# Attention's queries kept negated and scaled, and the sample's score products given two banks and a longer lag

## The chip, the core and the metric

The kernel runs on one core of a Trainium2 chip. The profile names the core's engines: PE (TensorE, the matmuls; PEld are its weight loads), DVE (VectorE), ACT (ScalarE), POOL (GpSimd) and SP (which here issues DMAs). Each engine works through its own list of instructions in a fixed order; an instruction that waits holds up all that stand behind it on its engine. The metric is the device time of one execution in microseconds (us); lower is better.

## The reference

One layer of a hybrid decoder for a prompt of 2048 tokens and for eight sample sequences with one new token each. Cut to what matters here:

```
h  = rms_norm(x) @ w_in                    # split into attention, indexer and recurrence parts
aq = rms_norm(aq, q_norm_g)                # 8 heads of 64; ak likewise with 2 heads
scores = sum_h relu(iq_h . ik) * iw_h      # indexer; keep the 256 best causal keys of each query
logits = (aq . ak_sel) * 64 ** -0.5        # masked where not chosen
att = softmax(logits) @ av_sel
x = x + concat(att, rec) @ w_out           # rec: a gated linear recurrence
x = x + square(relu(rms_norm(x) @ w_up)) @ w_down
```

For the samples the indexer scores 16384 cached keys of each of the eight sequences, picks 256 and gathers their keys and values.

## The kernel before

The prompt is 16 tiles of 128 rows (`NB`); the samples are one tile of 8 rows. The program runs in stages, and the trace shows their bounds:

- 0 to 1030 us: input projection, indexer scores of the prompt and the recurrence.
- Then three groups of tiles (0 to 4, 5 to 10, 11 to 15 with the samples). Each has an attention stage (from about 1030, 1885 and 2720 us) and an MLP stage with the output projection (from about 1280, 2095 and 2980 us). The first attention stage also holds the recurrence's share of the output projection.
- Beside the first two MLP stages run side tracks, generators advanced by so many matmul columns of the MLP (`PACE`, `PUMP`): the choice of the prompt's keys (`search_signs`, `choose`), and the samples' work (`sample`). The samples' indexer scores are all beside the first MLP stage, their choice, gathering and attention beside the second.

Products that need more than one pass are made of a high part and the rest: `wh`/`wl`, `uh`/`ul`, `kh`/`kl` and so on. ACT writes the high part, DVE (or POOL) subtracts it to get the low part.

**Prompt attention.** `logits` takes one head against all keys of a block in pieces of 512. Two matmuls make a piece in PSUM (`lg`, two banks); one DVE instruction adds the mask `MB`, writes `L` and carries the running maximum `mx`, which the core of the loop says:

```
front["dve"] = nc.vector.tensor_tensor_reduce(out=L[:, k0:k0 + kn], in0=ps[:, :kn], in1=MB[:, k0:k0 + kn],
                               scale=1.0, scalar=NEG if mx is None else mx,
                               op0=OP.add, op1=OP.max, accum_out=m2)
...
nm = p2.tile([P, 1], F32, tag="nm", name="nm", bufs=4)
nc.vector.tensor_scalar(nm, mx, -ATT_SCALE, None, op0=OP.mult)
nc.scalar.activation(L[:, :n], L[:, :n], AF.Exp, bias=nm, scale=ATT_SCALE, accum_out=sm[:, j:j + 1])
```

So each head of a block (16 blocks, 8 heads: 128 times) has a DVE instruction on one column (`nm`, L1001) between its last piece (L995) and its exponential on ACT (L1002). `values` then transposes `L` on PE (`pt`), splits it (`ph` on ACT, `pl` on DVE) and multiplies with the values (`O`).

**The samples' scores.** There are 32 units (8 sequences, 4 groups `u`). A unit gathers keys (`kg`, POOL), transposes them on DVE (`kt`, L1271) and makes four pieces: `kh` on ACT (L1282), `kl` on DVE (L1283), which `products` multiplies with the queries on PE (L1230), two matmuls a piece, summed over the four pieces in one PSUM bank `sc`. After that `weigh` copies half the bank on ACT (`rs`, L1237), adds the other half on DVE (`rs`, L1238), makes `rw` (L1239, L1240) and multiplies by the head weights (`wq`, L1242). `products` of a piece are written `LAG` pieces after its conversion; `kh` and `kl` have `LAG + 1` buffers; `sc` has `QS` banks. A bank is written anew only when the `rs` instructions of the unit that held it are done.

`LAG` also sets the delay of the products `lp` that build the samples' lists of keys (beside the second MLP stage), and `QS` the banks of other small products of the samples.

The order of instructions on every engine is made by a scheduler when the program is built, from priorities and the program's order, so a small edit moves many rows.

Of the kernel before, what the change touches and what calls it, by code (L numbers as in the profile page):

```python
# [8 lines left out]
F32 = mybir.dt.float32  # L9
# [8 lines left out]
OP = mybir.AluOpType  # L18
# [27 lines left out]
def hymba_kernel(ctx, tc, x_prompt, x_sample, cache_k, cache_v, cache_kidx, state_hgrn, page_table,  # L46
# [274 lines left out]
    def attn_proj(pc, p1, pr):  # L321
# [11 lines left out]
            nc.sync.dma_start(gains[:, i], src.to_broadcast([P, HD]))  # L333
        qg, kg, ig = (gains[:, i] for i in range(3))

        def load_weights(name, pieces):
            cols = sum(c for _, c in pieces)
            wh = p1.tile([P, 8, cols], F32R, name=f"wh_{name}")
            wl = p1.tile([P, 8, cols], F32R, name=f"wl_{name}")
            for q in range(4):  # L340
                raw = pr.tile([P, 2, 512], F32, tag="raw", name="raw", bufs=RB)
                d0 = 0
                for c0, c in pieces:
                    nc.sync.dma_start(raw[:, :, d0:d0 + c],
                                      w_in[0, q * 2 * P:(q + 1) * 2 * P, c0:c0 + c].rearrange("(k p) c -> p k c", p=P))
                    d0 += c
                s = slice(2 * q, 2 * q + 2)
                nc.scalar.copy(wh[:, s], raw[:, :, :cols])
                nc.vector.tensor_tensor(wl[:, s], raw[:, :, :cols], wh[:, s].bitcast(F32), op=OP.subtract)
            return wh, wl, cols  # L350
# [53 lines left out]
        def project_tile(t, po, q1, IK, hh, hl, i):  # L404
            n = rows(t)
            rs = slice(row0(t), row0(t) + n)
            for kind, (wh, wl, cols) in (("kiq"[i], weights[i]),):
# [3 lines left out]
                def post():  # L411
# [37 lines left out]
                            store(nv_sample[0].rearrange("b o k d -> (b o) (k d)"), o[:n, 128:256])  # L449
                            store(ni_sample[0].rearrange("b o d -> (b o) d"), o[:n, 256:320])  # L450
                    elif kind == "q":
                        head_norm(po, ps[:n], n, NH, qg, o[:n])
                        if t == NB:
                            store(aqD[rs], o[:n])
                            return
                        sp = split_heads(po, o, NH, "aqs", 1, nc.gpsimd)
                        for q in range(0, NH, 4):
                            pq = q1.tile([P, 512], F32, tag="ikt", name="aqt", bufs=2)
                            for j in range(4):
                                transpose_part(pq[:, j * P:(j + 1) * P], sp[:, q + j].rearrange("p a d -> p (a d)"))  # L460
                            qt = po.tile([P, 512], F32, tag="qt", name="qt", bufs=2)
                            (nc.vector.tensor_copy if q else nc.scalar.copy)(qt, pq)
                            store(qsD[t, :, q:q + 4], qt.rearrange("p (h t) -> p h t", t=P))
                    else:
                        nc.scalar.copy(o[:n], ps[:n])
                        store(iqD[rs], o[:n])
# [47 lines left out]
    def choose_keys(px):  # L514
# [25 lines left out]
        def choose(b, S, R):  # L540

            n = (b + 1) * P
            ngt, need = (small(x) for x in ("ngt", "need"))
            eq = px.tile([P, SEQ], BF, tag="eq", name="eq", bufs=1)
            nc.vector.tensor_scalar(eq[:, :n], S[:, :n], R, 0.0, op0=OP.is_gt, op1=OP.add, accum_out=ngt)

            ge, V, neq = (small(x) for x in ("ge", "V", "neq"))
            prev = -NEG
            for c in range(0, n, XC):
                cn = min(XC, n - c)  # L550
                tb = px.tile([P, XC], BF, tag="tb", name="tb", bufs=1)
                nc.vector.tensor_scalar(tb[:, :cn], S[:, c:c + cn], R, -NEG, op0=OP.is_le, op1=OP.mult)
                W = small("W")
                tj = px.tile([P, XC], BF, tag="rk", name="tj", bufs=1)
                nc.vector.tensor_tensor_reduce(out=tj[:, :cn], in0=tb[:, :cn], in1=S[:, c:c + cn], scale=1.0, scalar=prev,
                                               op0=OP.add, op1=OP.min, accum_out=W)
                prev = W
            gei = small("gei", I32)
            nc.vector.tensor_scalar(ge, ngt, float(TOPK), None, op0=OP.is_ge)
            nc.vector.tensor_copy(gei, ge)  # L560
            nc.vector.tensor_copy(V, R)
            nc.vector.copy_predicated(V, gei, W)
            nc.vector.tensor_scalar(eq[:, :n], S[:, :n], V, 0.0, op0=OP.is_equal, op1=OP.add, accum_out=neq)
            nc.vector.tensor_tensor(need, neq, ge, op=OP.mult)
            nc.vector.tensor_tensor(need, need, ngt, op=OP.subtract)
            nc.vector.tensor_scalar(need, need, float(TOPK), None, op0=OP.add)


            prev = 0.0
            for c in range(0, n, XC):  # L570
                cn = min(XC, n - c)
                s = slice(c, c + cn)
                rk = px.tile([P, XC], I16, tag="rk", name="rk", bufs=1)
                nc.vector.tensor_tensor_scan(rk[:, :cn], eq[:, s], eq[:, s], prev, op0=OP.add, op1=OP.max)
                if c + cn < n:
                    prev = small("prev")
                    nc.vector.tensor_copy(prev, rk[:, cn - 1:cn])
                cut = px.tile([P, XC], BF, tag="cut", name="cut", bufs=1)
                nc.vector.tensor_scalar(cut[:, :cn], rk[:, :cn], need, -2.0 ** -126, op0=OP.is_le, op1=OP.mult)
                MB = px.tile([P, XC], BF, tag="tb", name="MB", bufs=1)  # L580
                nc.vector.scalar_tensor_tensor(MB[:, :cn], S[:, s], V, cut[:, :cn], op0=OP.subtract, op1=OP.is_le)
                nc.vector.tensor_scalar(MB[:, :cn], MB[:, :cn], NEG, None, op0=OP.mult)
                store(mbD[b, :, s], MB[:, :cn])

        def choose_block(b, k):
# [363 lines left out]
    def attend_all(pk, blocks, rows_):  # L949
# [8 lines left out]
        def prep(p2, q2, cols, b, PT):  # L958
# [14 lines left out]
            if n > TOPK:  # L973
                nc.sync.dma_start(MB[:, :n], mbD[b, :, :n])
            else:
                nc.gpsimd.memset(MB[:, :n], 0.0)
                nc.gpsimd.affine_select(MB[:, b * P:n], MB[:, b * P:n], pattern=[[-1, P]], compare_op=OP.is_ge,
                                        fill=NEG, base=0, channel_multiplier=1)
            return aqT, MB

        def logits(p2, q2, cols, b, u, aqT, MB, LB, out):
# [4 lines left out]
            for j in range(2):  # L986
                L = p2.tile([P, cols], F32, tag="L", name="L", bufs=LB)
                mx = None
                for k0 in range(0, n, 512):
                    kn = min(512, n - k0)  # L990
                    ps = q2.tile([P, 512], F32, tag="lg", name="lg", bufs=2)
                    for i in range(2):
                        nc.tensor.matmul(ps[:, :kn], aqT[:, 2 * u + j], KS[k0 // 512][:, u // 2, i, :kn], start=i == 0, stop=i == 1)  # L993
                    m2 = p2.tile([P, 1], F32, tag="mx", name="mx", bufs=8)
                    front["dve"] = nc.vector.tensor_tensor_reduce(out=L[:, k0:k0 + kn], in0=ps[:, :kn], in1=MB[:, k0:k0 + kn],  # L995
                                                   scale=1.0, scalar=NEG if mx is None else mx,
                                                   op0=OP.add, op1=OP.max, accum_out=m2)
                    mx = m2
                    yield
                nm = p2.tile([P, 1], F32, tag="nm", name="nm", bufs=4)  # L1000
                nc.vector.tensor_scalar(nm, mx, -ATT_SCALE, None, op0=OP.mult)  # L1001
                nc.scalar.activation(L[:, :n], L[:, :n], AF.Exp, bias=nm, scale=ATT_SCALE, accum_out=sm[:, j:j + 1])  # L1002
                out.append(L)

        def values(p2, q2, b, u, att, PTB, OB, sm, *Ls):
# [78 lines left out]
        return attention  # L1084


    QT, QS = 1, 1
    LAG, REST, KGB, RWB = 2, 4, 4, 1

    def sample():  # L1090
        with tc.tile_pool(name="p4", bufs=1, side="right", reuse_waits="tile") as p4:
# [700 lines left out]
```

## Time and profile before

| | us |
|---|---|
| three runs | 3516.57, 3520.95, 3522.51 (median 3520.95) |
| the profiled execution: time, span from first to last instruction | 3515.95, 3514.2 |
| busy PE, PEld, DVE, ACT, POOL | 3315.7, 2912.1, 2345.8, 2202.5, 1201.2 |
| mean granted TensorE clock | 0.977 of full speed |

Busy time is the time in which an engine runs an instruction. The rest of PE's span, some 198 us, is waiting; the trace tells for each wait which instruction ended it. The granted clock is 1 at 2.4 GHz and 0.5 at 1.2 GHz. The share of an engine is an average over stages with different limits, so the stages are read one by one.

### The profile page before, as it was taken

The numbers are of one execution on the slowest core, as the hardware profiler recorded it, in microseconds if no ns is written. First come the engines' busy times: TensorE is split into PE (matmuls) and PEld (weight loads), VectorE is DVE, ScalarE is ACT, GpSimd is POOL, SyncE is SP. The second block draws the span as 40 slices with busy tenths as digits, with TensorE's granted clock in tenths as the row PEclk, the third lists the DMA queues.
The fourth block names the chain that finished last, engine by engine and source line by source line (L and its number), as shares of the span: only waits on it lengthen the run. The fifth ranks groups of instructions, "written<-read, shape, count | busy, mean of one in ns | idle before, by whom it ended". The sixth has DMA issues, their size and how long they took to land. (4 is left out here: it accounts for less than half of the span.)

```text
span 3514.2 us, 56706 instructions
## 1 busy us (share of the span) xinstructions
PE 3315.7 (94%) x20230; PEld 2912.1 (83%) x20230; DVE 2345.8 (67%) x5150; ACT 2202.5 (63%) x4063; POOL 1201.2 (34%) x1460
## 2 busy tenths in 40 slices
PE   8999889999998989989999988999999999999999
PEld 7787788999996778877787778888989788888888
DVE  3577788877684358898795788796384787322323
ACT  5789887777674258858844665765973576333332
POOL 5565776655544035554442101042211000100000
PEclk9999999999999999999999999999999999999999
DMA  6564647464535446555546112334336201444443
GB/s 212 156 177 146 176 144 194 139 165 133 163 104 192 146 133 209 190 170 167 168 148 223 36 59 88 126 100 163 130 127 226 84 25 37 150 144 141 135 136 129
DMA packets 343244, 499.95 MB, mean 142 GB/s; under 512 B 38536, under 2 KB 252144, under 8 KB 341936
## 3 DMA queue, kind: packets, MB, share of 16 engines
q1 hardware_dynamic: 280784, 326.35, 29.4%
q0 software_dynamic: 62176, 169.96, 15.8%
q8 instruction: 159, 2.61, 0.3%
q14 instruction: 125, 1.02, 0.1%
HBM read 374.26 MB, written 121.96 MB: 141 GB/s over the span
## 5 line engine op out<-in xcount | busy, mean ns | idle before, releaser
L528 ACT ACTIVATE jkA<-S,candA 128x1664 int8<-128x1664 f32 (+11 forms) x448 | 586.3, 1310 | 116.8 <-DVE candA L532 101.4
L1748 DVE TENSOR_TENSOR y<-y,dn 128x512 f32<-128x512 f32 x512 | 346.5, 683 | 342.9 <-PE dn L129 339.7
L127 PE MATMUL up<-hh,wh 128*128 128x384 f32 (+2 forms) x1536 | 496.5, 323 | 4.7 <-ACT wh L1570 3.5
L128 PE MATMUL up<-hl,wh 128*128 128x384 f32 (+2 forms) x1536 | 496.2, 323 | 0.0
L129 PE MATMUL up<-hh,wl 128*128 128x384 f32 (+2 forms) x1536 | 491.2, 323 | 4.6 <-DMA wl<-low 3.2
L128 PE MATMUL dn<-dl,uh 128*128 128x512 f32 x1024 | 407.8, 398 | 6.0 <-POOL dl L1574 3.4
L127 PE MATMUL dn<-dh,uh 128*128 128x512 f32 x1024 | 404.5, 399 | 4.8 <-DVE y L1748 4.2
L129 PE MATMUL dn<-dh,ul 128*128 128x512 f32 x1024 | 402.2, 396 | 5.3 <-DVE ul L1724 5.0
L127 PEld LDWEIGHTS up<-hh,wh 128*128 128x128 f32 x1536 | 294.9, 192 | 18.2 <-ACT wh L1570 4.9
L128 PEld LDWEIGHTS up<-hl,wh 128*128 128x128 f32 x1536 | 294.7, 192 | 13.5 <-issue 3.9
L129 PEld LDWEIGHTS up<-hh,wl 128*128 128x128 f32 x1536 | 294.5, 192 | 13.0 <-DMA wl<-low 4.8
L1570 ACT CAST dh<-raw 128x1024 fp32r<-128x1024 f32 x96 | 96.8, 1047 | 284.0 <-PE dn L129 276.7
L129 PEld LDWEIGHTS dn<-dh,ul 128*128 128x128 f32 x1024 | 194.9, 191 | 49.0 <-DVE ul L1724 6.8
L506 DVE SCALAR_TENSOR_TENSOR sl<-ix,iw,sl 128x512 f32<-128x512 f32 (+3 forms) x266 | 180.4, 678 | 78.0 <-ACT ix L502 75.5
L127 PEld LDWEIGHTS dn<-dh,uh 128*128 128x128 f32 x1024 | 193.8, 190 | 42.9 <-DVE y L1748 6.7
L128 PEld LDWEIGHTS dn<-dl,uh 128*128 128x128 f32 x1024 | 195.1, 191 | 38.8 <-POOL dl L1574 4.3
L1724 DVE TENSOR_TENSOR ul<-rl,uh 128x384 fp32r<-128x384 f32 x192 | 114.3, 597 | 157.2 <-ACT uh L1723 155.9
L500 PE MATMUL ix<-IK,iqT 128*128 128x512 f32 (+3 forms) x608 | 187.1, 393 | 28.7 <-DVE sl L506 19.7
L1572 POOL DMA_DIRECT2D dl<-low x64 | 34.9, 545 | 521.9 <-PE dn L129 477.9
L502 ACT ACTIVATE ix<-ix,iw 128x512 f32<-128x512 f32 (+3 forms) x304 | 182.3, 604 | 48.5 <-PE ix L500 45.4
L993 PE MATMUL lg<-KS,aqT 128*128 128x512 f32 (+3 forms) x640 | 195.9, 402 | 14.5 <-DVE mx L995 10.7
L1269 POOL DMA_INDIRECT kg<-in_cache_kidx_dram,pti x128 | 132.3, 1033 | 210.7 <-DVE kt L1271 180.1
(498 smaller groups left out, 9330.6 us busy)
## 6 DMA issues: line engine op xcount, KB each, us to landing
raw<-in_w_up_dram SPq DMA_DIRECT2D x96, 512.0 KB
raw<-in_w_down_dram SPq DMA_DIRECT2D x96, 512.0 KB
wl<-low POOLq DMA_DIRECT2D x72, 512.0 KB
raw<-in_w_in_dram SPq DMA_DIRECT2D x256, 128.0 KB
dl<-low POOLq DMA_DIRECT2D x64, 512.0 KB
wl<-lowp POOLq DMA_DIRECT2D x48, 512.0 KB
low<-wl SPq DMA_DIRECT2D x40, 512.0 KB
low<-dl SPq DMA_DIRECT2D x32, 512.0 KB
```

The source lines that it names most:

```text
L127: nc.tensor.matmul(ps, lh, rh, start=first, stop=False)
L128: nc.tensor.matmul(ps, lh, rl, start=False, stop=False)
L129: nc.tensor.matmul(ps, ll, rh, start=False, stop=last)
L500: nc.tensor.matmul(ps[:, :kn], iqT[:, h], IK[:, i, k0:k0 + kn], start=i == 0, stop=i == 1)
L502: nc.scalar.activation(r[:, :kn], ps[:, :kn], AF.Relu, scale=iw[:, 1, h:h + 1])
L506: nc.vector.scalar_tensor_tensor(sl, r[:, :kn], iw[:, 2, h:h + 1], sl, op0=OP.mult, op1=OP.add)
L528: nc.scalar.activation(jk[:, :n], S[:, :n], AF.Sign, bias=cand.bitcast(F32), scale=-1.0, accum_out=cnt)
L993: nc.tensor.matmul(ps[:, :kn], aqT[:, 2 * u + j], KS[k0 // 512][:, u // 2, i, :kn], start=i == 0, stop=i == 1)
L1269: nc.gpsimd.indirect_dma_start(out=kg_, out_offset=None, in_=kview, in_offset=bass.IndirectOffsetOnAxis(ap=pti[:, b, g, u:u + 1], axis=0))
L1570: nc.scalar.copy(wh, raw)
L1724: nc.vector.tensor_tensor(ul[:, o], rl[:, :cn], uh[:, o].bitcast(F32), op=OP.subtract)
L1748: front["dve"] = nc.vector.tensor_tensor(ys_[t][:, s], ys_[t][:, s], po, op=OP.add)
```

## The change

It does three things.

- The gain that multiplies the prompt's normed queries is replaced by one times minus `ATT_SCALE` (`qn`, made once on POOL). The products with the keys are then the logits, scaled and negated. The mask adds +3e38 in place of -3e38, the reduction keeps the minimum, and the exponential takes scale -1 and the running minimum itself as its bias. The 128 `nm` instructions go. The sample tile keeps the plain gain.
- `QS` goes from 1 to 2: `sc` has two banks.
- `LAG` goes from 2 to 4: four pieces between a conversion and its products, and five buffers in place of three for `kh` and `kl`, and for `oh` and `ol` of the list products.

```
+        qn = pc.tile([P, HD], F32, name="qn")
+        nc.gpsimd.tensor_scalar(qn, qg, -ATT_SCALE, None, op0=OP.mult)
...
-                        head_norm(po, ps[:n], n, NH, qg, o[:n])
+                        head_norm(po, ps[:n], n, NH, qn if t < NB else qg, o[:n])
...
-                nc.vector.tensor_scalar(MB[:, :cn], MB[:, :cn], NEG, None, op0=OP.mult)
+                nc.vector.tensor_scalar(MB[:, :cn], MB[:, :cn], -NEG, None, op0=OP.mult)
...
-                                        fill=NEG, base=0, channel_multiplier=1)
+                                        fill=-NEG, base=0, channel_multiplier=1)
...
-                                                   scale=1.0, scalar=NEG if mx is None else mx,
-                                                   op0=OP.add, op1=OP.max, accum_out=m2)
+                                                   scale=1.0, scalar=-NEG if mx is None else mx,
+                                                   op0=OP.add, op1=OP.min, accum_out=m2)
...
-                nm = p2.tile([P, 1], F32, tag="nm", name="nm", bufs=4)
-                nc.vector.tensor_scalar(nm, mx, -ATT_SCALE, None, op0=OP.mult)
-                nc.scalar.activation(L[:, :n], L[:, :n], AF.Exp, bias=nm, scale=ATT_SCALE, accum_out=sm[:, j:j + 1])
+                nc.scalar.activation(L[:, :n], L[:, :n], AF.Exp, bias=mx, scale=-1.0, accum_out=sm[:, j:j + 1])
...
-    QT, QS = 1, 1
-    LAG, REST, KGB, RWB = 2, 4, 4, 1
+    QT, QS = 1, 2
+    LAG, REST, KGB, RWB = 4, 4, 4, 1
```

The built programs differ in order from the first attention stage on; the last MLP stage and, but for `qn`, all before 1030 us stand as they stood. Lines behind the first edit have moved by up to three numbers in the changed file.

DVE, first MLP stage, one unit of the samples' scores. Before, three `kl` of a unit stand in a row, then `rs` of the unit ahead of it, and the fourth `kl` further down:

```order
L1283 TENSOR_TENSOR kl_17335<-kt_17278,kh_17334 128x512
L1283 TENSOR_TENSOR kl_17341<-kt_17278,kh_17340 128x512
L1283 TENSOR_TENSOR kl_17405<-kt_17278,kh_17404 128x512
L1238 TENSOR_TENSOR rs_17410<-sc_17187,rs_17410 64x512
L1724 TENSOR_TENSOR ul_17435<-rl_17461,uh_17434 128x384
L529 TENSOR_SCALAR incA0_15650<-cntA0_17466 128x1
L532 SCALAR_TENSOR_TENSOR candA0_15649<-incA0_15650,candA0_15649 128x1
L1240 SCALAR_TENSOR_TENSOR rw_17411<-rs_17410,rw_17411 64x512
L529 TENSOR_SCALAR incA1_15660<-cntA1_17471 128x1
L532 SCALAR_TENSOR_TENSOR candA1_15659<-incA1_15660,candA1_15659 128x1
L1283 TENSOR_TENSOR kl_17429<-kt_17278,kh_17428 128x512
L1748 TENSOR_TENSOR y_15489<-y_15489,dn_17592 128x512
```

In the changed program the `rs` row reads the unit two ahead, stands behind the first `kl`, and the other three `kl` follow close on it:

```order
L1284 TENSOR_TENSOR kl_17465<-kt_17376,kh_17464 128x512
L1749 TENSOR_TENSOR y_15415<-y_15415,dn_17571 128x512
L532 TENSOR_SCALAR incA1_15582<-cntA1_17458 128x1
L1239 TENSOR_TENSOR rs_17470<-sc_17095,rs_17470 64x512
L535 SCALAR_TENSOR_TENSOR candA1_15581<-incA1_15582,candA1_15581 128x1
L1284 TENSOR_TENSOR kl_17489<-kt_17376,kh_17488 128x512
L1284 TENSOR_TENSOR kl_17527<-kt_17376,kh_17526 128x512
L1284 TENSOR_TENSOR kl_17533<-kt_17376,kh_17532 128x512
L1749 TENSOR_TENSOR y_15415<-y_15415,dn_17579 128x512
L1272 STREAM_TRANSPOSE kt_17564<-kg_17565 128x16x32
```

The `rs` row moved up past two `kl` rows, and the fourth `kl` moved up to its fellows.

PE, first MLP stage, the products of those same pieces. Before, the first three pieces are six matmuls in a row (the fourth piece stands 27 rows further down):

```order
L127 MATMUL up_17523<-hh_13756,wh_17354 128x256
L1230 MATMUL sc_17333<-kh_17334,BQ0_15598 128x512
L1230 MATMUL sc_17333<-kl_17335,BQ0_15598 128x512
L1230 MATMUL sc_17333<-kh_17340,BQ0_15598 128x512
L1230 MATMUL sc_17333<-kl_17341,BQ0_15598 128x512
L1230 MATMUL sc_17333<-kh_17404,BQ0_15598 128x512
L1230 MATMUL sc_17333<-kl_17405,BQ0_15598 128x512
L128 MATMUL up_17523<-hl_13757,wh_17354 128x256
L129 MATMUL up_17523<-hh_13756,wl_17355 128x256
```

In the changed program all four pieces of a unit stand within ten rows here, with single rows of the MLP between:

```order
L127 MATMUL dn_17601<-dh_17502,uh_17421 128x512
L1231 MATMUL sc_17463<-kh_17464,BQ0_15520 128x512
L1231 MATMUL sc_17463<-kl_17465,BQ0_15520 128x512
L1231 MATMUL sc_17463<-kh_17488,BQ0_15520 128x512
L1231 MATMUL sc_17463<-kl_17489,BQ0_15520 128x512
L1231 MATMUL sc_17463<-kh_17526,BQ0_15520 128x512
L128 MATMUL dn_17601<-dl_17503,uh_17421 128x512
L1231 MATMUL sc_17463<-kl_17527,BQ0_15520 128x512
L1231 MATMUL sc_17463<-kh_17532,BQ0_15520 128x512
L129 MATMUL dn_17601<-dh_17502,ul_17422 128x512
L1231 MATMUL sc_17463<-kl_17533,BQ0_15520 128x512
L129 MATMUL up_17676<-hh_13758,wl_17667 128x384
```

What moved is the fourth piece, up to the other three.

DVE, third attention stage, the end of one head. Before:

```order
L995 ISA L_34245,mx_34303<-lg_34300,MB_33335,mx_34285 128x512
L995 ISA mx_34303 128x1
L1024 TENSOR_TENSOR pl_34199<-pt_34193,ph_34198 128x512
L1024 TENSOR_TENSOR pl_34217<-pt_34211,ph_34216 128x512
L1001 TENSOR_SCALAR nm_34316<-mx_34303 128x1
L1024 TENSOR_TENSOR pl_34235<-pt_34229,ph_34234 128x512
L1024 TENSOR_TENSOR pl_34257<-pt_34251,ph_34256 128x512
L995 ISA L_34334,mx_34338<-lg_34335,MB_33335 128x512
L995 ISA mx_34338 128x1
```

The row `nm`, and its 127 fellows, are gone from the changed program.

## Rows read from the trace of the kernel before

**Rows 1.** Busy time by engine in the seven stages (PEclk: granted clock).

```profile
core 0: us, PE busy (x) PEld busy (x) DVE busy (x) ACT busy (x) POOL busy (x), PEclk, DMA share, GB/s
0.00:1030.00 1030.00, 962.97 (x6691) 868.88 (x6692) 744.71 (x1604) 787.37 (x1684) 616.64 (x768) 0.98 0.58 162
1030.00:1280.00 250.00, 237.48 (x1354) 185.62 (x1353) 114.48 (x338) 115.20 (x260) 62.84 (x77) 1.00 0.45 151
1280.00:1885.00 605.00, 553.59 (x2927) 489.49 (x2926) 514.41 (x948) 426.78 (x740) 295.70 (x204) 0.95 0.57 182
1885.00:2095.00 210.00, 194.08 (x1203) 156.85 (x1201) 158.46 (x452) 136.61 (x265) 24.05 (x55) 0.99 0.19 63
2095.00:2720.00 625.00, 598.87 (x3527) 542.57 (x3528) 439.21 (x1010) 403.61 (x556) 119.31 (x163) 0.98 0.41 137
2720.00:2980.00 260.00, 246.60 (x1577) 206.34 (x1576) 206.54 (x529) 166.04 (x276) 24.78 (x49) 0.98 0.14 46
2980.00:3514.00 534.00, 522.12 (x2961) 462.36 (x2959) 167.98 (x273) 166.93 (x284) 57.89 (x144) 0.99 0.42 140
```

**Rows 2.** Whom PE waited for, whole span: us in total, times, longest.

```profile
PE sc L1230 <- DVE kl L1283: 11.1, 4, 4.4
PE lg L993 <- DVE mx L995: 10.7, 26, 2.4
PE sc L1230 <- DVE rs L1238: 10.1, 4, 4.0
...
PE O L1032 <- DVE pl L1024: 5.4, 18, 1.1
PE dn L129 <- DVE ul L1724: 5.0, 2, 3.1
...
PE sc L1230 <- DVE need L566: 4.4, 1, 4.4
PE pt L1016 <- ACT L L1002: 4.0, 3, 3.4
...
PE sc L1230 <- DVE incA L529: 2.2, 1, 2.2
```

**Rows 3.** The tile nm: count, ns min/median/max, and who waited for it.

```profile
L1001 DVE TENSOR_SCALAR nm<-mx x128: 134/150/155, 1060.4 to 2958.6; 128x1 f32<-128x1 f32 x128
...
  ACT L L1002: 38.0, 48
```

**Rows 4.** Timeline of one stall: start, us taken, engine, line, idle before.

```profile
1609.96 6.63 DVE L1283 TENSOR_TENSOR kl<-kt,kh 128x512 fp32r<-128x512 f32 x3
1610.14 4.69 POOL L1574 TENSOR_TENSOR dl<-raw,dh 128x1024 fp32r<-128x1024 f32 x2
...
1616.52 0.68 DVE L1238 TENSOR_TENSOR rs<-sc,rs 64x512 f32<-64x512 f32 x1
...
1617.25 0.80 PE L1230 MATMUL sc<-kh,BQ 128*128 128x512 f32 x1 [2.25 <-DVE incA L529]
```

**Rows 5.** Tile kl in the first MLP stage: ns min/median/max.

```profile
L1283 DVE TENSOR_TENSOR kl<-kt,kh x125: 670/685/7206, 1279.5 to 1851.4; 128x512 fp32r<-128x512 f32 x125
```

**Rows 6.** The same stage's groups by shape: busy us, mean ns, idle before.

```profile
L1283 DVE TENSOR_TENSOR kl<-kt,kh 128x512 fp32r<-128x512 f32 x125 | 127.5, 1042 | 14.0 <-ACT kh L1282 10.7 <-ACT rl L1721 1.9 <-PE sc L1230 0.7
```

**Rows 7.** Whom ACT waited for, whole span.

```profile
ACT rs L1237 <- PE sc L1230: 19.8, 5, 6.7
...
ACT kh L1282 <- PE sc L1230: 5.1, 5, 1.9
```

**Rows 8.** A short stretch behind a wait for rs, columns as in the first group.

```profile
1490.00:1493.50 3.50, 3.50 (x17) 3.28 (x16) 1.50 (x6) 3.50 (x8) 0.00 (x0) 0.53 0.84 293
```

**Rows 9.** POOL's timeline at the start of the program.

```profile
5.70 0.56 POOL L119 TENSOR_TENSOR rx<-rx,neghalf 128x1 f32<-128x1 f32 x1
7.52 2.35 POOL L391 TENSOR_TENSOR xt<-xt,g 128x1024 f32<-128x1024 f32 x1 [1.26 <-ACT xt L390]
```

**Rows 10.** Store of the samples' attention.

```profile
L1559 SPq DMA_DIRECT2D attD<-ao x8: 263/292/295, 2633.4 to 2635.7; - x8
```

## The prediction

> **What bounds the kernel now.** I read the stages first. PE is busy for 94% of the span, and in no stage is another engine busier than PE [rows 1]; the reader should see how far PE's busy time stays below the length of its stage. That is 12.5, 15.9 and 13.4 us in the three attention stages, together 41.8, and 51.4 us in the first MLP stage (605 less 553.6). That MLP stage has the samples' scores beside it, the busiest DVE of the longer stages (514 of 605 us, 85%) and the lowest granted clock, 0.95. So the kernel is a queue of matmuls that stops for short waits, and what the change is worth is the part of these waits that it removes.
>
> Then I read whom PE waited for. Waits of the score products `sc` are 11.1 and 4.4 us for `kl` (the second is put down to `need`, which stands beside `kl` in DVE's work of that time), and 10.1 and 2.2 us for `rs` (the second is put down to `incA`, just behind it): 27.8 us, all in the first MLP stage, more than half of its 51.4. In the attention stages the names to look for are `lg` on `mx` with 10.7 us in 26 waits, `O` on `pl` with 5.4 in 18, and `pt` on the exponentials with 4.0 in 3: 20.1 us [rows 2].
>
> One stall shows how such a wait comes about. Three `kl` take 6.63 us while POOL subtracts two weight tiles for 4.69 us, `rs` stands behind them, and the product starts when `rs` is done, 2.25 us late [rows 4]. A `kl` takes 0.685 us in the median, 7.2 at worst [rows 5], and 1.042 on average [rows 6]: over 125 of them DVE loses 125 x 0.357 = 45 us to such stretches. A wait also costs clock: in the 3.5 us after a wait for `rs` the granted clock was 0.53, so near its level of 1.2 GHz [rows 8].
>
> **Part by part.** The sum starts from the profiled execution's own 3515.95 us; it lies 5.0 us below the median of the runs, 3520.95, and I carry the difference over unchanged.
>
> *The nm instructions.* 128 of 150 ns go, 19.2 us of DVE, and the exponential starts that much earlier [rows 3]. DVE is not the bound of these stages (114, 158 and 207 us busy of 250, 210 and 260) [rows 1], so most of it is hidden behind matmuls. The cover is gone only where PE waits for DVE or the exponential: 47 waits, 20.1 us [rows 2]. That is the upper bound, and zero the lower. If each of the 47 had one `nm` ahead of it, 47 x 0.15 = 7 us would go; there are 128 `nm` to 320 pieces, so less than every second has one, but one removed `nm` also helps pieces behind it. I take 4 us. What is late next there is the piece's own DVE instruction, which stays.
>
> *The second bank.* A product that opens a unit had to wait for `rs` of the unit before it, now for that of the unit two before. But the order moved `rs` as well: it stands in the second unit after its own, behind one `kl` where it stood behind three. So the wait is not gone, it is shorter by two `kl`: 2 x 0.685 = 1.37 us [rows 5]. In the stall shown the product would have waited 0.9 us in place of 2.25 [rows 4]. Five such waits with 12.3 us [rows 2] give 5 x 1.37 = 7 us.
>
> *Four pieces behind.* The fourth `kh` of a unit waited for a buffer that the products of the first piece held: ACT waited 5.1 us for `sc` there, and 19.8 us for `sc` before `rs` [rows 7]. With five buffers it does not, and its `kl` moves up to the other three. The five waits for `kl`, 15.5 us [rows 2], fall behind that piece or behind a `kl` that POOL holds up. But DVE has the same work at 85% load and PE's list puts the products close behind the pieces again, so the lag shows in the program and hardly in the order. I take a quarter, 4 us; the bounds are nothing and 15.5.
>
> The Trainium skill, on its page SBUF — State Buffer, section Who interferes with whom, speaks against these two terms: a VectorE instruction with two inputs in SBUF and a GpSimd instruction that reads SBUF share a port pair by an exclusive lock, and the loser fully blocks. `kl` reads `kt` and `kh`, and the trace agrees (three `kl` in 6.63 us beside POOL's 4.69). By that rule alone neither a bank nor a lag shortens a `kl`, and both terms would be nothing.
>
> *Clock.* At 0.95 the first MLP stage lacks 5% of 605, 30 us of full-speed time [rows 1]. The `sc` waits are 27.8 of its 51.4 us of waiting, so I lay 16 us to them. Of these waits 7 + 4 of 27.8 go, 40%, and 40% of 16 is 6 us. So the samples' part is 7 + 4 + 6 = 17 us, between nothing and 27.8 + 16 = 44.
>
> *What else the edits touch.* The lists' products get the same lag and end two steps of at most 9000 columns later. The first MLP stage has about 1.04 million columns by the code (61,440 of `w_out`, 491,520 each of `up` and `dn`) in its 605 us [rows 1], so two steps are some 10 us; the samples' attention is stored at 2633 us [rows 10] and read from 2980 us: nothing. `qn` stands on POOL between `rx`, done at 6.26, and the product of the first tile, which starts at 7.52 after an idle time of 1.26 us [rows 9]. The longest that such a small POOL instruction takes there is 0.56 us, so it is hidden unless its gain arrives late; bounds 0 and 0.6, taken as 0. Gain, mask and minimum replace operations of the same shape: nothing. The scheduler deals the attention stages and the second MLP stage anew with the same work; I take 0 and allow 5 us either way, about a third of what PE waits in one attention stage.
>
> **Sum.** 4 + 17 = 21 us: 3516 - 21 = 3495 for the profiled execution, and 3521 - 21 = 3500 for the median of runs.
>
> **The rivals.** *The products wait as before.* The stalls come from POOL holding `kl`, POOL's subtractions are unchanged, and the products stand just behind the pieces. For it speaks the stall above, and that the average `kl` is 0.36 us over its median; against it, that `rs` stood behind three of them and now behind one. Only the 4 us of `nm` are left: 3517. (The page of the Trainium skill named above, SBUF — State Buffer, leads to this case.) Within 0.2% (7 us, about what a measurement of this kernel can tell from no change) that is the same. Chance 0.19.
>
> *Slower: pieces in front of the MLP's own low parts.* The fourth `kl`, 1.04 us on average, now runs ahead of a `ul`, two steps of the choice and an `rw` that stood before it. `dn` needs `ul`, and PE waited for it only twice, 5.0 us [rows 2]. Each `ul` that comes too late costs about 1.04 us and then some 1.6 us of clock (47% of 3.5 us) [rows 8], so 2.6. The stage has 64 `ul`. It decides from (21 + 7) / 2.6, so eleven late ones, on; with one in each second of the 32 units and half a `kl` of queue more, 16 x 3, it is 48 - 21 = 27 us slower: 3548. For it speaks DVE's 85%; against it, that the fourth `kl` has to be done at some time and that its wait blocked PE as well. Chance 0.17.
>
> *All of it goes.* Each unit's loop (`rs`, products, conversion, `rs`) now spans two units, so DVE's delays of some 5 us are taken up and no `sc` waits: 44 + 4, so 3473. Against it speaks that the order keeps the products close. Chance 0.09.
>
> **How the numbers follow.** The forecast, a gain of 7 to 40 us around 21, has the chance 0.55. Faster by over 0.2% is that and the last rival, 0.64; the same 0.19; slower 0.17. The range reaches up to 3528, the edge of the same with some of the slower case in it, and down to 3475, which holds the forecast whole and leaves out the last rival's lower half and the upper half of the slower one: about 0.8. Of the forecast alone it is 3481 to 3514.
>
> **What would show it.** Right: the first MLP stage about 588 us, `sc` waits of PE some 17 us with those for `rs` the most reduced, its granted clock 0.96; each attention stage 1 to 2 us shorter; 128 fewer DVE instructions; a `kl` still at about 1.04 us on average. Wrong: `sc` waits of 25 us or more (the first rival), new waits of `dn` for `ul` (the second), or an attention stage that changes by more than 5 us, which would be the new order's doing and which I could not price.

## The result: slower by 0.5%, and the profile after

The changed kernel takes 3534.79 us in the median of 6 runs (3530.99 to 3541.1), beside it the kernel before 3520.05 (6 runs); the ratio of all the runs is 1.0052, 95% interval 1.0042 to 1.0062 (the quotient of the two medians is 1.0042). Its profiled execution is the second longest of its runs, 3540.88 us, and that of before the shortest, 3515.95. So the two traces differ by 25 us where the medians differ by 15; stages are read from traces, totals from ratios.

The stages of after, to be laid beside [rows 1] (busy time by engine; the later windows are moved along with the program):

```profile
1280.00:1890.00 610.00, 551.84 (x2930) 486.50 (x2929) 505.96 (x941) 424.51 (x737) 290.40 (x204) 0.95 0.56 181
1890.00:2102.00 212.00, 194.52 (x1201) 156.27 (x1199) 153.59 (x404) 138.32 (x267) 24.02 (x55) 0.99 0.18 61
2102.00:2742.00 640.00, 605.00 (x3531) 548.15 (x3532) 444.64 (x1011) 403.84 (x557) 116.52 (x164) 0.97 0.41 134
2742.00:3005.00 263.00, 247.13 (x1575) 205.10 (x1574) 202.01 (x489) 166.06 (x275) 24.00 (x49) 0.98 0.13 44
```

The second MLP stage takes 640 us in place of 625 for the same matmuls, the first 610 in place of 605, at the same granted clock of 0.95. The third attention takes 263 in place of 260. DVE has its 128 instructions less, in all 5022.

Windows at round numbers blur such differences, so from here on a stage runs from the end of one milestone to the next: the last `O` of an attention, the last `dn` of an MLP (the first attention begins at its first product `lg`, at 1059 us; the third MLP runs to the end). From before to after: first attention 193.5 and 193.5, first MLP 643.8 and 648.4, second attention 190.2 and 192.7, second MLP 648.7 and 663.0, third attention 238.4 and 242.2, third MLP 540.3 and 540.3. Of the 25 us, 14.3 lie in the second MLP stage, to which the prediction gave 0.

Whom PE waited for in the first MLP stage of after (us in total, times, longest), to be laid beside [rows 2]:

```profile
PE dn L127 <- DVE y L1749: 19.1, 5, 15.1
PE dn L129 <- DVE ul L1725: 6.5, 3, 3.6
...
PE up L127 <- ACT rl L1722: 4.5, 4, 2.6
PE sc L1231 <- DVE incA L532: 4.4, 3, 2.7
PE up L127 <- ACT wh L1571: 3.8, 3, 2.7
PE dn L127 <- ACT uh L1724: 3.5, 2, 2.4
PE sc L1231 <- DVE rs L1239: 3.1, 3, 2.7
...
PE sc L1231 <- DVE kl L1284: 1.5, 2, 1.2
```

The waits of the score products fell from 27.8 us to 9.0, more than forecast. In their place stand waits of the MLP's own products, one of them 15.1 us long. The scores end at 1824 us, 28 us earlier than before (1852).

That one wait is a chain through five queues. Timeline of after (start, us, engine, operation, idle before and its releaser), SP's queue first:

```profile
1833.03 6.55 SPq L135 DMA_DIRECT2D mbD<-MB  x2
1844.00 0.80 SPq L977 DMA_DIRECT2D MB<-mbD  x2
1844.89 0.38 SPq L1586 DMA_DIRECT2D raw<-in_w_up_dram  x1
...
1839.57 0.58 POOL L968 DMA_DIRECT2D KS<-ksD  x1
...
1857.12 1.04 ACT L1571 CAST wh<-raw 128x1024 fp32r<-128x1024 f32 x1 [13.03 <-DMA raw<-in_w_up_dram]
1858.07 0.41 ACT L1723 ACTIVATE rl<-rl 128x256 f32<-128x256 f32 x1
1858.52 0.41 ACT L1724 CAST uh<-rl 128x256 fp32r<-128x256 f32 x1
...
1858.95 1.91 DVE L1725 TENSOR_TENSOR ul<-rl,uh 128x256 fp32r<-128x256 f32 x1 [10.42 <-ACT uh L1724]
1860.79 1.87 DVE L1749 TENSOR_TENSOR y<-y,dn 128x512 f32<-128x512 f32 x3
...
1861.52 0.80 PE L127 MATMUL dn<-dh,uh 128*128 128x512 f32 x1 [15.10 <-DVE y L1749]
```

Read it from the end. PE waits for a `dn` bank that `y` frees; `y` stands on DVE behind a `ul`, which waits for `uh`; `uh` stands on ACT behind a conversion `wh`, which waits for the last `w_up` load. A buffer for that load came free when POOL's subtraction was done, at 1839.0; but in SP's queue two mask stores and the read back of the masks into the next attention (`MB<-mbD`) stood ahead, so it was issued at 1844.9. And the next attention's queries, keys and values had started from 1839.0 on (the first keys at 1839.6), eight transfers, 5.4 MB; keys and values take over the samples' buffers, which the last `wq` product frees. In the trace of before the same load goes out ahead of them:

```profile
1845.89 0.38 SPq L1585 DMA_DIRECT2D raw<-in_w_up_dram  x1
...
1853.46 1.04 ACT L1570 CAST wh<-raw 128x1024 fp32r<-128x1024 f32 x1
...
1861.92 0.55 POOL L965 DMA_DIRECT2D KS<-ksD  x1 [4.40 <-PE wq L1242]
```

There the conversion runs 7.6 us after the issue, and ACT does not wait for the load; in after it runs 12.2 us after, and ACT waits 13.0 us for it. What the stall costs besides its 15.1 us stands in the windows of after (columns as in [rows 1]):

```profile
1846.00:1858.00 12.00, 0.42 (x2) 0.00 (x0) 2.54 (x1) 0.88 (x1) 2.25 (x1) 0.65 1.12 389
1850.00:1867.00 17.00, 5.48 (x13) 4.37 (x14) 4.40 (x6) 1.77 (x3) 2.34 (x1) 0.51 1.11 388
```

The DMA engines are busy all the time (share 1.11 and 1.12), at 389 GB/s, and TensorE has 17 us at a granted clock of 0.51, its level of 1.2 GHz; about 5 of these 17 us lie behind the wait.

### The profile page after: what moved, and what is told of

The parts are those of the page before. It is cut to its first block, busy times and chain, and to the rows that moved or that the text cites. A ratio compares the mean times of both kernels' runs of the same rounds, so it can differ in the third digit from the quotient of the medians.

```text
span 3539.2 us, 56553 instructions
## 1 busy us (share of the span) xinstructions
PE 3321.6 (94%) x20230; PEld 2911.9 (82%) x20230; DVE 2335.4 (66%) x5022; ACT 2204.1 (62%) x4063; POOL 1191.6 (34%) x1461
## 5 line engine op out<-in xcount | busy, mean ns | idle before, releaser
L531 ACT ACTIVATE jkA<-S,candA 128x1664 int8<-128x1664 f32 (+12 forms) x448 | 586.2, 1310 | 142.3 <-DVE candA L535 114.7
L127 PEld LDWEIGHTS dn<-dh,uh 128*128 128x128 f32 x1024 | 194.4, 190 | 73.0 <-DVE y L1749 30.1
L1725 DVE TENSOR_TENSOR ul<-rl,uh 128x384 fp32r<-128x384 f32 x192 | 129.2, 673 | 178.5 <-ACT uh L1724 177.3
L996 PE MATMUL lg<-KS,aqT 128*128 128x512 f32 (+3 forms) x640 | 197.4, 403 | 13.9 <-DVE mx L998 11.8
```

The lines of the kernel that those rows point to most:

```text
L127: nc.tensor.matmul(ps, lh, rh, start=first, stop=False)
L531: nc.scalar.activation(jk[:, :n], S[:, :n], AF.Sign, bias=cand.bitcast(F32), scale=-1.0, accum_out=cnt)
L1725: nc.vector.tensor_tensor(ul[:, o], rl[:, :cn], uh[:, o].bitcast(F32), op=OP.subtract)
```

## The experiments

Each kernel stood beside runs of the kernel before on the same chip; the ratio is to these. The stages (us) are from each kernel's profile, one execution each. Up to the first `lg` all kernels have the same program but for `qn`, and there their profiles take 1058.2 to 1063.8 us: a difference of some 5 us in one stretch of two profiles can be chance.

| kernel | ratio (95% interval) | median | first MLP | second attention | second MLP | third attention |
|---|---|---|---|---|---|---|
| before | 1 | 3520 to 3524 | 643.8 | 190.2 | 648.7 | 238.4 |
| after | 1.0052 (1.0042 to 1.0062) | 3534.8 | 648.4 | 192.7 | 663.0 | 242.2 |
| nm_only | 1.0009 (1.0000 to 1.0018) | 3521.4 | 636.3 | 194.1 | 647.2 | 241.3 |
| bank_only | 1.0025 (1.0016 to 1.0035) | 3528.1 | 647.7 | 192.1 | 647.6 | 238.0 |
| lag_only | 1.0063 (1.0050 to 1.0076) | 3541.6 | 646.4 | 193.1 | 659.8 | 236.7 |
| bank_lag | 1.0061 (1.0048 to 1.0074) | 3539.4 | 648.6 | 190.5 | 659.0 | 238.3 |
| keys_late | 1.0033 (1.0021 to 1.0045) | 3530.4 | 627.6 | 194.1 | 666.7 | 242.8 |
| pump7300 | 1.0008 (0.9997 to 1.0020) | 3523.0 | 617.1 | 195.6 | 663.5 | 243.1 |
| list2 | 1.0038 (1.0024 to 1.0053) | 3533.5 | 649.4 | 192.9 | 648.6 | 240.6 |
| late_list2 | 0.9992 (0.9983 to 1.0000) | 3516.9 | 626.3 | 196.6 | 651.9 | 240.9 |
| pump_list2 | 0.9963 (0.9951 to 0.9975) | 3508.0 | 618.8 | 195.6 | 650.1 | 241.7 |
| pump_list2_nm | 0.9941 (0.9929 to 0.9953) | 3501.8 | 620.5 | 192.8 | 648.9 | 238.1 |
| before_pump | 0.9975 (0.9964 to 0.9986) | 3513.4 | 628.5 | 199.2 | 648.4 | 238.4 |
| nm_idle | 1.0008 (0.9998 to 1.0018) | 3526.0 | 634.8 | 198.4 | 647.7 | 241.7 |
| before_late | 0.9999 (0.9987 to 1.0010) | 3521.7 | 643.9 | 191.5 | 651.3 | 237.6 |
| late_list2_nm | 0.9968 (0.9958 to 0.9978) | 3510.2 | 630.0 | 192.0 | 650.7 | 237.3 |

**The parts one by one.** The attention part alone (after with `QS = 1`, `LAG = 2`), and the samples' part on the kernel before:

```
-    QT, QS = 1, 1
-    LAG, REST, KGB, RWB = 2, 4, 4, 1
+    QT, QS = 1, 2                       (bank_only, bank_lag)
+    LAG, REST, KGB, RWB = 4, 4, 4, 1    (lag_only, bank_lag)
```

> Only the attention part of the change: negated queries, minimum, no nm; one bank and products two pieces behind as before. Theory Q (the loss comes from the samples' part, whose scores end earlier, so that the choice's mask stores hold up weight loads in the loads' queue): this kernel gains 0 to 7 us on before, 3513 to 3520, the first MLP stage keeps its 28 us of sc waits and no new wait of 15 us. Theory N (taking nm away deals the attention stages and what follows them anew, and that costs): 5 to 12 us slower, with attention stages 2 to 4 us longer as in the changed kernel.

> Only the second bank for the sample scores. Theory Q: the sc waits for rs fall from 12 us to a few, the scores end some 10 us earlier, so the end of the first MLP stage may or may not meet the late weight load: 3505 to 3525. Theory N: the attention stages stay as before to within 1 us and the time is 5 to 10 us below before.

> Only the lag of four pieces (score products and list products). Theory Q: the sc waits for kl fall, the scores end some 15 us earlier, and the second MLP stage (list products four pieces behind) carries part of the loss: 3515 to 3530. Theory N: attention stages as before, 0 to 10 us faster.

> Second bank and lag of four, attention as before (with nm). Theory Q: scores end some 28 us earlier as in the changed kernel, a new wait of 10 us or more near the end of the first MLP stage, that stage 3 to 6 us longer and the second MLP stage some 10 us longer: 3528 to 3538. Theory N: sc waits below 10 us without that loss, first MLP stage 15 us shorter, attention stages as before: 3500 to 3510.

The attention part alone lies at or just above before, so most of the loss is elsewhere, but it is no gain either: it misses the 3520 of theory Q by little, and theory N's 5 to 12 us are too many, though its three attention stages are longer, as theory N had it (197.7, 194.1 and 241.3 us for 193.5, 190.2 and 238.4). Bank and lag together give the whole loss, with a wait of 14.8 us at 1854 us like that of after. That is theory Q's mechanism; its ranges were too low for all three. Each edit alone takes away the `sc` waits it was meant for, and gets others: with the bank those for `rs` are gone and `dn` waits 12.0 us for `y`, with the lag those for `kl` are gone and `dn` waits 19.4 us for `y`, 11 times; the first stage stays at 646 to 648 in both. The lag's 3541.6, where at most 3530 was expected, comes with a second MLP stage of 659.8, as in bank_lag, while with the bank alone it stays at 647.6.

**The two hold-ups.** keys_late puts queries, keys, values and masks of the next attention behind the last `w_up` block in the issue order of POOL and of SP, and changes nothing else:

```
             if name == "w":
+                last["pool"], last["sp"] = front["pool"], dma
...
+            for x in last.values():
+                behind.enter_context(tc.issue_after(x.ins))
             nc.gpsimd.dma_start(aqT, qsD[b])
```

pump7300 makes the samples' steps in the first stage rarer, and list2 gives the lists' products their own lag:

```
-    PACE, PUMP = (12000, 14000), (7000, 9000)
+    PACE, PUMP = (12000, 14000), (7300, 9000)
...
-                        if len(pending) > LAG:       (list products, and bufs of oh, ol)
+                        if len(pending) > LAG2:      (LAG2 = 2)
```

> The changed kernel, but the next attention's keys, values and queries (POOL's queue) and its masks (SP's queue) are issued behind the last w_up block of the MLP. Theory H (the 15.1 us wait is a late w_up load, held behind a mask store and its read back in SP's queue, and slowed beside 3.4 MB of keys and values): that load is issued some 5 us earlier and lands within 8 us, the 15 us wait and its 17 us at half clock go, the first MLP stage is 20 to 24 us shorter (about 626), the time 3509 to 3517. Rival M (the MLP waits for DVE and ACT wherever they are late, and a wait taken away comes back at the next product): the stage stays above 640, the time 3527 to 3537.

> The changed kernel with the samples' steps 4% slower (one per 7300 columns in place of 7000), so that the scores end some 20 us later, near where they ended before. Theory H: keys and values then start behind the last w_up load by themselves, the 15 us wait goes, stage about 630, the time 3513 to 3522. Rival M: the same waits move with the steps, 3530 to 3540.

> The changed kernel, but the products of the samples' key lists (second MLP stage) two pieces behind again; only the score products stay four behind. If the lists' lag makes the second MLP stage longer (659 to 663 against 647 to 649 with a lag of two), that stage returns to 646 to 651, the first stays as it is, the time 3520 to 3526. If it is only the new order or chance, the second stage stays at 655 or more, the time 3531 to 3538.

> Both of these edits on the changed kernel: keys, values and masks behind the last w_up block, lists' products two behind. If both causes are right the two gains add: 3496 to 3506, faster than the kernel before by 0.4 to 0.7%. If the waits only move: 3518 to 3526.

(The volume in the first of these texts is too small; the eight transfers move 5.4 MB.) With late keys the first stage falls from 648.4 to 627.6 us, as theory H had it, and the trace shows why:

```profile
1841.02 0.38 SPq L1593 DMA_DIRECT2D raw<-in_w_up_dram  x1
1842.92 0.32 SPq L981 DMA_DIRECT2D MB<-mbD  x1
...
1852.32 0.58 POOL L972 DMA_DIRECT2D KS<-ksD  x1
...
1846.93 1.04 ACT L1576 CAST wh<-raw 128x1024 fp32r<-128x1024 f32 x1
```

The load goes out 3.9 us earlier than in after, in a stage that began 6 us later, ahead of the masks' read back, and its conversion starts 5.9 us behind it; the 15 us wait is gone. The edit moves the load and the transfers beside it at once, so it does not tell which of the two held the load up more. With slower steps the keys start behind the load by themselves (1844.5 us, the load at 1821.6) and the stage is 617.1 (the total, 3523.0, is 1 us above its range); how much of that is the keys' doing, the control before_pump below tells. The total of keys_late missed its range (3530 for at most 3517). Its profile is 9.0 us shorter than that of after, not 21: the first MLP stage begins 6.1 us later, 3.1 of them from the stretch up to the first `lg`, and the second MLP stage takes 3.7 us more. After's profiled execution is also 6 us above its own median.

The second MLP stage answers to the lists' lag. In five kernels with a lag of four it takes 659.0 to 666.7 us, in the eleven with two 647.2 to 651.9, before included. Its waits in after and in list2:

```profile
PE up L127 <- ACT wh L1571: 4.7, 3, 3.6
PE dn L127 <- DVE y L1749: 4.4, 2, 2.7
...
PE up L129 <- DMA wl<-low: 4.1, 3, 2.1
PE dn L128 <- DMA dl<-low: 2.5, 1, 2.5
```

```profile
PE dn L128 <- DMA dl<-low: 2.3, 2, 1.3
PE up L129 <- DMA wl<-low: 1.8, 1, 1.8
...
PE dn L127 <- DVE y L1750: 1.1, 1, 1.1
```

The list step lasts two steps longer, from the first list product to the last 98 us in place of 87, and the choice's passes on ACT and DVE, a weight conversion behind them, fall on other places of the MLP. PE waits 39.3 us in that stage of after and 30.1 in list2, with a granted clock of 0.97 and 0.98. So a handful of waits of 1 to 4 us and their clock make 14 us; which of them comes from the longer list step was not tried one by one. list2 as a whole gains only 0.14% on after and misses its range (3533.5 for at most 3526), though its stage came back as expected; beside keys_late, late_list2 gains 13.5 us by the same edit. Part of the difference is chance: the profile of list2 is 7.0 us shorter than after's where its second MLP stage is 14.4 shorter, and the other way go 6.4 us before the first MLP stage, 4.5 of them up to the first `lg`. The rest is open. late_list2, 3516.9, lies between its two ranges: its two stages are about as short as with one edit each (626.3 and 651.9), the total is 11 us above the range in which the gains add.

**Slower steps and short lists together, nm put back, and two controls.** pump_list2 is both edits on after; pump_list2_nm the same with the attention of before; before_pump changes the one number in the kernel before; nm_idle still computes `nm` and lets the exponential read `mx`:

```
+                nm = p2.tile([P, 1], F32, tag="nm", name="nm", bufs=4)
+                nc.vector.tensor_scalar(nm, mx, -ATT_SCALE, None, op0=OP.mult)
                 nc.scalar.activation(L[:, :n], L[:, :n], AF.Exp, bias=mx, scale=-1.0, accum_out=sm[:, j:j + 1])
```

> The changed kernel with the samples' steps 4% slower (7300 columns) and the lists' products two pieces behind. If the two losses are separate (first stage 617 with the slower steps, second stage 648 with the lag of two) they add: 3523 less 15, so 3505 to 3512, faster than before by 0.2 to 0.5%. If the second stage's loss only follows the order of the first: 3518 to 3524.

> The same with the attention as before the change (nm computed, maximum kept): only the samples' part changed. If taking nm away lengthened the attention stages by 3 us each (241 to 243 against 237 to 238 in the third, 193 to 196 against 190 to 193 in the second), this is 4 to 8 us faster than the kernel with nm removed, 3499 to 3506. If the attention's growth is chance: the same time to within 2 us.

> The kernel before with nothing but the slower steps (7300). It tells whether the short first stage belongs to the second bank and the lag or to the slower steps by themselves. If to bank and lag: sc waits stay near 25 us, first stage 635 to 645, 3515 to 3522. If to the steps alone: first stage about 620, 3495 to 3505.

> The attention part of the change alone, with the nm instruction still computed and nothing reading it: DVE has its 128 instructions, the exponentials wait for the minimum only. If DVE's work were what counted, this is slower than without nm by up to 4 us, and if the exponential's earlier start counted, faster than before by as much. If the order of the matmuls counts (it is nearly that of the kernel without nm), the attention stages are as long as there, and the time 3519 to 3526.

The two repairs add, 3508.0, inside the range for separate losses. Putting the attention of before back gains another 6.2 us, as expected: 3501.8, 0.59% faster than before and the fastest kernel here. The control tells that slower steps help the kernel before too, by 0.25%; neither answer of its expectation fits, it lies between. Its first MLP stage is 15.3 us shorter, without bank or lag, so pump7300's short stage is not the keys' doing alone. And 9.0 us of it come back in the second attention stage (199.2 us), whose first wait for `mx` is 9.8 us in place of 2.4: a short stage is to be read with the next one.

nm_idle is as fast as nm_only, and its third attention (241.7 us) is as long. So the 128 DVE instructions cost nothing measurable. What nm_idle and nm_only share is the order of the matmuls: in the third attention 1414 of 1477 matmuls stand at the same place in both, and 945 in before and nm_only. So the 4 us probably come with the order; a kernel with the minimum in the old order, which would show it, was not built. In all eight kernels with the maximum and `nm` the third attention takes 236.7 to 238.4 us, in the eight with the minimum 240.6 to 243.1. Its opening shows both halves, ACT of before and of nm_only:

```profile
2741.07 1.04 ACT L1570 CAST wh<-raw 128x1024 fp32r<-128x1024 f32 x1 [5.16 <-DMA raw<-in_w_out_dram]
2742.03 1.57 ACT L1002 ACTIVATE L<-L,nm 128x1536 f32<-128x1536 f32 x1
...
2750.16 1.58 ACT L1002 ACTIVATE L<-L,nm 128x1536 f32<-128x1536 f32 x1
```

```profile
2742.13 1.04 ACT L1571 CAST wh<-raw 128x1024 fp32r<-128x1024 f32 x1 [5.58 <-DMA raw<-in_w_out_dram]
2743.08 1.57 ACT L1003 ACTIVATE L<-L,mx 128x1536 f32<-128x1536 f32 x1
...
2751.04 1.58 ACT L1003 ACTIVATE L<-L,mx 128x1536 f32<-128x1536 f32 x1 [0.88 <-DVE mx L998]
```

The stage's longest wait, for the first exponential, is not ended by `nm` at all: the exponential stands behind a conversion that waits for a load. And the third one, which followed without a pause, now waits 0.88 us for `mx`, since the pieces are dealt in another order. The first MLP stage of nm_only and nm_idle, in which nothing was edited, is 7 to 9 us shorter than that of before, and the total still longer: the three attention stages together take 11.0 and 12.9 us more. Why the MLP stage is shorter stays open.

**What bank and lag are worth with nothing held up.** The late keys on the kernel before, and on it with bank, lag of four and lists two behind.

> The kernel before with keys, values and masks of the next attention behind the last w_up block, nothing else. If the hold-up came only with the scores' earlier end: no change, 3517 to 3524. If late keys help by themselves: 3505 to 3514.

> Attention as before; second bank, score products four behind, list products two behind; keys, values and masks late. Theory G (bank and lag gain what was forecast, 17 us, when nothing behind them is held up): 3501 to 3508, first MLP stage about 626. Theory S (they gain about half, the rest of a short first stage is the pace or chance): 3509 to 3516.

Late keys by themselves change nothing, and the first stage of before comes out again at 643.9 us. Against it bank and lag take 11.5 us (3521.7 to 3510.2; stage 643.9 to 630.0): theory S. At the slower pace the same step is 11.6 us, before_pump to pump_list2_nm. The first stage of before; of before_late and late_list2_nm; of before_pump and pump_list2_nm (columns as in [rows 1]):

```profile
1253.00:1897.00 644.00, 591.22 (x3177) 523.57 (x3178) 536.91 (x1019) 446.11 (x774) 306.48 (x225) 0.95 0.56 181
```

```profile
1252.60:1896.50 643.90, 589.37 (x3175) 522.33 (x3176) 536.28 (x1019) 445.68 (x773) 302.02 (x224) 0.95 0.56 180
1254.00:1884.00 630.00, 578.49 (x3177) 511.09 (x3174) 526.29 (x1019) 445.18 (x773) 300.19 (x224) 0.98 0.57 184
```

```profile
1255.50:1884.00 628.50, 583.10 (x3175) 516.32 (x3176) 519.53 (x1020) 446.74 (x773) 301.77 (x224) 0.96 0.56 181
1256.00:1876.00 620.00, 583.21 (x3173) 515.50 (x3172) 517.34 (x1019) 445.83 (x771) 309.66 (x224) 0.96 0.57 187
```

PE hardly waits less in late_list2_nm: 51.5 us (630.0 less 578.5), for 54.5 in before_late and 52.8 in before. Nearly the whole gain there, 10.9 us, is in PE's busy time, at a clock of 0.98 in place of 0.95. At the slower pace it is the other way: PE waits 36.8 us for 45.4, and busy time and clock stay as they were. And nm_only, without bank or lag, has 580.8 us of busy time at 0.96 in this stage, so a part of such a clock gain can come with a new order or by chance.

## Why the prediction was wrong

It forecast 3500, a gain of 21 us, and a range of 3475 to 3528; measured is a loss of 15 by the medians. From before to after the ratios of the experiments make a chain: bank and lag -0.31% (before_late to late_list2_nm), `nm` away +0.24% (to late_list2), the two hold-ups back +0.60% (to after), late keys -0.01%; together the 0.52%, some 18 us. The links were measured at different times, each beside its own runs of before. Of the two hold-ups, the late load is worth 0.19% by itself (after to keys_late) and the lists' lag 0.14% (after to list2), both together 0.60%, more than the sum; why is open.

*The second bank, four pieces behind, clock: 17 us.* Right in sign, too large: 11.5 us in both settings. The step that failed is that a `sc` wait taken away is PE time won. The `sc` waits fell by more than the 11 us forecast, to 9.0 us (13.0 in late_list2_nm), but in late_list2_nm PE's waiting fell by only 3.0 us and the clock term, put at 6 us, was nearly all of the gain; at the slower pace waiting fell by 8.6 us and the clock term was nothing. So the split between waits and clock is not a fixed one. DVE and ACT are still late; in late_list2_nm most of the waits now fall on the MLP:

```profile
PE up L127 <- ACT wh L1576: 7.8, 4, 2.7
PE sc L1236 <- DVE incA L530: 6.7, 2, 4.1
...
PE dn L127 <- ACT uh L1731: 4.8, 3, 2.4
PE up L127 <- ACT rl L1729: 4.7, 5, 2.6
PE dn L129 <- DVE ul L1732: 4.5, 2, 3.6
```

DVE's groups in the first MLP stage tell the same, after first, then before:

```profile
L1284 DVE TENSOR_TENSOR kl<-kt,kh 128x512 fp32r<-128x512 f32 x128 | 103.4, 831 | 0.8 <-ACT kh L1283 0.6
...
L1725 DVE TENSOR_TENSOR ul<-rl,uh 128x256 fp32r<-128x256 f32 x32 | 33.2, 1037 | 16.0 <-ACT uh L1724 15.9
```

```profile
L1283 DVE TENSOR_TENSOR kl<-kt,kh 128x512 fp32r<-128x512 f32 x128 | 129.5, 1033 | 14.3 <-ACT kh L1282 11.1 <-ACT rl L1721 1.9 <-PE sc L1230 0.7
...
L1724 DVE TENSOR_TENSOR ul<-rl,uh 128x256 fp32r<-128x256 f32 x32 | 21.3, 665 | 1.1 <-ACT uh L1723 1.1
```

The forecast that a `kl` stays at 1.04 us [rows 6] was wrong: it fell to 0.83, and `ul` rose from 0.67 to 1.04. DVE's busy time in the stage fell by only 6.0 us (536.9 to 530.9), while all `kl` took 26.1 us less: `ul` of both widths took 14.1 more and the choice's `candA` 10.7 more. So most of the stretches in which POOL holds DVE up moved from the pieces to the MLP's low parts and the choice. In both kernels 34 instructions of `kl`, `ul`, `candA` and `rw` take over 1.5 times their group's median, and every one of them overlaps a subtraction of POOL. Three `rs` of each kernel overlap one too and stay at 0.68 us; `rs` has one input in SBUF, the other in PSUM. This agrees with what the Trainium skill says on its page SBUF — State Buffer, section Who interferes with whom: a VectorE instruction with two inputs in SBUF contends with a GpSimd instruction that reads SBUF, and the order of issue, not the operation, decides who blocks.

*The nm instructions: -4 us.* Wrong in sign in three comparisons, +0.09, +0.22 and +0.24%, 3 to 8 us slower; a fourth, bank_lag to after, gives -0.09%, with intervals that overlap. In all four the third attention stage gets longer, by 2.9 to 3.9 us. The step that failed is "if each of the 47 had one `nm` ahead of it, 47 x 0.15": the longest waits were ended by pieces and by a load, and nm_idle, which keeps the 128 instructions, is no slower than nm_only. `O` waits for `pl` and `lg` for `mx` 6.9 and 11.8 us in all of after, for 5.4 and 10.7 before.

*"The scheduler deals the attention stages and the second MLP stage anew with the same work; I take 0 and allow 5 us either way"*, and the lists' lag, "nothing". These are the steps that failed most. The third attention lost 4 us, probably to the new order, and the second MLP stage 14 to the lists' lag, which was taken as nothing because its result is needed late. (It is: the store [rows 10] moved to 2661 us, and its first product stands at 3001.6 us; the fetch of it, which the prediction put at 2980 us, goes out at 2731.5, in before at 2710.3.) What the lag displaced beside it was not asked.

*Not in the sum at all:* what the scores' earlier end sets free. The samples' buffers go to the next attention's keys, and with them 5.4 MB of transfers move 22 us up, in front of the last weight load. That wait and its clock cost about 20 us of stage (648.4 to 627.6: 16.6 us of waiting, 4.2 of busy time).

*The rivals.* "The products wait as before" is refuted by the 9.0 us of `sc` waits. "Slower: pieces in front of the MLP's own low parts" had the sign, and `ul` did become slower, but `dn`'s waits for it grew only from 5.0 to 6.5 us; most of the loss has other places. "All of it goes" fell with the first term. `qn` on POOL ran from 6.89 to 7.29 us and the first tile's product started at 7.53, before at 7.52 [rows 9]: hidden, as forecast.

## What to carry to other kernels

A wait of the busiest engine names where a late helper engine was met, not what it is worth to move: ask which instruction the same lateness will hit next, and change the helper's load or pace (one number, the pace, gave 0.25% here) before the buffers. When side work ends earlier, look at what its freed memory starts, and which transfers of the main work are then behind it in a queue; an ordering edge that keeps the prefetch behind the last weight load took 16.6 us here (list2 to late_list2), more than bank and lag gain, though 4.4 us with the lists' lag still in (after to keys_late) and nothing on the kernel before. And a shared constant such as `LAG` is one edit per user: give each user its own, and price each.

## What the runs showed of the hardware

The last `w_up` load, 512 KB, was converted 5.9 us (keys_late) and 7.6 us (before) after its issue; in after it was 12.2 us, with ACT waiting for it, beside 5.4 MB of prefetch and at 389 GB/s for all. And the granted clock does not follow the sum of the waits: the first MLP stage shows 0.95 with 52.8 us of waiting, 0.98 with 51.5 and 0.96 with 36.8. Which sequence of waits costs how much clock was not settled by these runs.
